# Seven products of halves instead of eight in the up-projections of a ConvFFN, on one Trainium2 core

## The chip, the cores and the metric

The kernel runs on one core of one Trainium2 chip. The metric is the time of one execution in microseconds of device time. Times of stretches are counted from the first instruction of the profiled execution.

## The reference, cut to what matters

Two layers (a hybrid of attention and linear attention, then a short convolution) process 512 prompt tokens and 32 sample tokens, 544 columns together. Each layer ends in a ConvFFN, and this is where the change lies:

```python
D_FF = ((8 * D_MODEL // 3 + 127) // 128) * 128     # 2816, D_MODEL = 1024

def conv_ffn(h, w_up, conv_w, conv_b, w_down, past):
    u = h @ w_up                                   # (tokens, 2 * D_FF)
    uc, new = causal_dwconv(u, past, conv_w)       # three taps along the tokens
    gate, val = jnp.split(uc + conv_b, 2, axis=-1)
    return (jax.nn.gelu(gate, approximate=True) * val) @ w_down, new
```

## The kernel before

Features lie on partitions, tokens along the free axis, in float32. Each product is made as three matmuls of float32r: weights and activations are split into a high part (`wh`, `xh`) and the rest (`wl`, `xl`), and high by high, high by low and low by high are summed in PSUM (`mm3`). The tokens are two halves of 256 and 288 columns.

Weights come in jobs of 128 x 1024 floats: SP issues the DMA into `wr`, ACT copies to `wh` (L193), DVE subtracts to get `wl` (L196); `prepare` runs two jobs ahead of the products.

The ConvFFN (`ffn`, L1546) has 22 pairs of a gate block and a value block of 128 features each. They are done in parts of 5, 5, 4, 4 and 4 pairs (`PARTS`). In a part, the up-projection of each pair runs (two jobs of 48 matmuls each, `run`), its epilogue `ev` multiplies by the norm, does the three taps on ACT and DVE (L1580 to L1582), the gelu, the product of gate and value (L1589) and its split (L411, L412) into `gh` and `gl`. Then the down-projection of the part runs over these: eight blocks, whose contraction goes over the pairs of the part. So the first matmuls of a down-projection need the first pair's `gh` and `gl`, the last ones of each block the last pair's.

The tensor engine's products use five PSUM banks (`pg`). POOL (GpSimd) only prepares margins: it clears and fills the history columns of `u` (L1569, L1570) and copies out the new state (L1578), and it adds squares for the norms.

The order on each engine is set at build time by the framework's scheduler. An engine then works through its instructions in that order; each waits for its operands and holds up those behind it.

Of the kernel before, what the change touches and what calls it, by code (L numbers as in the profile page):

```python
# [32 lines left out]
PARTS = (5, 5, 4, 4, 4)  # L33
# [52 lines left out]
def tile_hybrid_step(  # L86
# [65 lines left out]
    def sm_(w=256, s="m"):  # L152
        return apool.tile([P, w], F32, tag="m", name=nm(s), bufs=3)
# [27 lines left out]
    loaders = []  # L181
# [3 lines left out]

    def prepare(upto, eng=V):
        while len(wready) <= min(upto, len(loaders) - 1):
            n, load = loaders[len(wready)]
            wr = wpool.tile([P, 8 * P], F32, tag="wr", name=nm("wr"), bufs=2)
            wl = wpool.tile([P, 8 * P], F32R, tag="wl", name=nm("wl"))  # L190
            wh = wpool.tile([P, 8 * P], F32R, tag="wh", name=nm("wh"))
            load(wr)
            ins = S.activation(wh[:, :n], wr[:, :n], AF.Copy)  # L193
            if hold:
                behind(ins, hold[0])
            ins = eng.tensor_tensor(wl[:, :n], wr[:, :n], wh[:, :n].bitcast(F32), ALU.subtract)  # L196
            if vhold and eng is V:
                behind(ins, vhold[0])
            if load is load_glr:
                wk, lk = (t.rearrange("p (k c) -> p k c", k=8) for t in (wh, wl))  # L200
                eng.tensor_copy(wk[:, :, 16:32], lk[:, :, 0:16])
            wready.append((wh, wl))

    def cols(w, c0, r0=0, nkb=8):
        n = 2 * P if nkb == 4 else P

        def load(wr):
            nc.sync.dma_start(
                wr[:, : nkb * n].rearrange("p (k c) -> p k c", k=nkb),
                w[r0 : r0 + nkb * P, c0 : c0 + n].rearrange("(k p) c -> p k c", p=P),  # L210
            )
# [24 lines left out]
    def behind(ins, first):  # L236
        """keeps ins behind first in its engine's order"""
# [7 lines left out]
    def fence(ins, us):  # L245
        """ins goes ahead of the products that come more than us microseconds from here"""
# [29 lines left out]

# [1511 lines left out]
```

## Time and profile before

| | |
|---|---|
| time, median of 3 runs | 1328.41 us (1327.65 to 1331.36) |
| span of the profiled execution, first to last instruction | 1323.4 us |
| its own time outside the span | not listed; the median is 5.0 us above the span |
| PE / DVE / ACT / POOL busy | 97% / 63% / 42% / 18% |

PE is TensorE's matmuls, DVE is VectorE, ACT is ScalarE, POOL is GpSimd. In a timeline the first column is the start, the second the duration; where a row has "x2", both instructions are in one row. The distance between the starts of two instructions that follow each other without idle time is what one costs its engine.

### The profile page before, as it was taken

Reading aid. Unit: us, or ns where it says so; the run is one execution under the profiler, and the core shown is the slowest. Engines: PE = TensorE matmul, PEld = TensorE weight load, DVE = VectorE, ACT = ScalarE, POOL = GpSimd, SP = SyncE. Lnnn points to the kernel's source line nnn. Section 1 sums busy time; section 2 is a strip of 40 time slices with the busy share of each in tenths; the row PEclk is TensorE's granted clock in tenths of the full one; section 3 lists DMA queues with packets and bytes.
Section 4 is the critical chain, followed back from the end, with each engine's and each line's share of the span. In section 5 each row is a group of like instructions: output and inputs, shape, how many; then the busy total and the mean of one; then the engine's idle time right before and its main releaser. Section 6 shows DMA issues by size and latency. Waiting matters only on the chain.

```text
span 1323.4 us, 25024 instructions
## 1 busy us (share of the span) xinstructions
PE 1290.0 (97%) x10094; PEld 1253.5 (95%) x10094; DVE 839.3 (63%) x1692; ACT 561.8 (42%) x1070; POOL 233.9 (18%) x469
## 2 busy tenths in 40 slices
PE   7999999989999999999998999998999999999997
PEld 6999887888999999999998999998999999999997
DVE  6487466477837657575778645428755656657566
ACT  6555456644543334242445322335444323333244
POOL 4110210153301001020244000035120101001013
PEclk9999999999999999999999999999999999999999
DMA  6422221222242242323221432321333233232311
GB/s 213 112 51 67 85 74 35 68 64 75 61 138 73 76 125 80 96 80 96 80 81 39 120 96 80 103 70 37 104 89 112 61 107 105 81 96 80 96 45 69
DMA packets 199982, 113.14 MB, mean 85 GB/s; under 512 B 13805, under 2 KB 198218, under 8 KB 199850
## 3 DMA queue, kind: packets, MB, share of 16 engines
q1 hardware_dynamic: 194114, 106.99, 27.7%
q10 hardware_dynamic: 5304, 3.38, 0.8%
q8 instruction: 79, 1.29, 0.4%
q0 software_dynamic: 448, 1.18, 0.3%
q14 instruction: 37, 0.30, 0.1%
HBM read 107.07 MB, written 5.47 MB: 85 GB/s over the span
## 4 chain that ended last, share of the span: by engine, by line
PE 90%; DVE 7%; issue 1%; DMA 0%; POOL 0%; ACT 0%; SPq 0%; POOLq 0%; DVEq 0%; ACTq 0%
PE pg L225 27%; PE pg L230 27%; PE pg L232 27%; DVE m L536 2%; DVE xl L552 2%; PE ps L178 2%; DVE xres L540 2%; PE ps L1240 1%; PE ps L968 1%; PE ps L1301 1%; DMA sink<-attn_sinks 0%; PE ps L306 0%; DVE m L491 0%; PE ps L318 0%; PE ps L1178 0%
## 5 line engine op out<-in xcount | busy, mean ns | idle before, releaser
L225 PE MATMUL pg<-xh,wh 128*128 128x256 f32 (+1 forms) x2048 | 593.0, 291 | 5.3 <-DVE m L491 3.6
L230 PE MATMUL pg<-xl,wh 128*128 128x256 f32 (+1 forms) x2048 | 592.1, 289 | 2.8 <-DVE xl L552 2.4
L232 PE MATMUL pg<-xh,wl 128*128 128x256 f32 (+1 forms) x2032 | 586.4, 289 | 0.0
L225 PEld LDWEIGHTS pg<-xh,wh 128*128 128x128 f32 x2048 | 387.1, 190 | 8.4 <-issue 5.4
L230 PEld LDWEIGHTS pg<-xl,wh 128*128 128x128 f32 x2048 | 388.0, 189 | 4.4 <-DVE xl L552 3.0
L232 PEld LDWEIGHTS pg<-xh,wl 128*128 128x128 f32 x2032 | 384.2, 189 | 1.0 <-issue 0.9
L193 ACT ACTIVATE wh<-wr 128x1024 fp32r<-128x1024 f32 (+1 forms) x203 | 204.5, 1009 | 375.2 <-PE pg L230 272.2
L196 DVE TENSOR_TENSOR wl<-wr,wh 128x1024 fp32r<-128x1024 f32 (+1 forms) x197 | 228.1, 1159 | 142.4 <-ACT wh L193 140.7
L230 PE MATMUL pg<-gl,wh 128*128 128x256 f32 (+1 forms) x704 | 200.8, 288 | 0.0
L232 PE MATMUL pg<-gh,wl 128*128 128x256 f32 (+1 forms) x704 | 200.3, 288 | 0.0
L225 PE MATMUL pg<-gh,wh 128*128 128x256 f32 (+1 forms) x704 | 195.4, 289 | 0.0
L1578 POOL COPY uc<-u 128x18 f32<-128x18 f32 x88 | 51.7, 588 | 602.5 <-DVE u L1577 602.5
L230 PEld LDWEIGHTS pg<-gl,wh 128*128 128x128 f32 x704 | 132.3, 188 | 0.2
L232 PEld LDWEIGHTS pg<-gh,wl 128*128 128x128 f32 x704 | 132.3, 188 | 0.0
L225 PEld LDWEIGHTS pg<-gh,wh 128*128 128x128 f32 x704 | 129.1, 188 | 0.0
L1574 DVE TENSOR_TENSOR u<-pg,nbc 128x256 f32<-128x256 f32 x88 | 36.8, 423 | 113.6 <-PE pg L232 113.6
L491 DVE TENSOR_TENSOR m<-m,pg 128x256 f32<-128x256 f32 (+1 forms) x144 | 58.8, 434 | 57.1 <-PE pg L232 56.8
L1580 ACT ACTIVATE y<-u,cw 128x560 f32<-128x560 f32 x88 | 74.1, 849 | 20.2 <-DVE u L1577 20.1
L411 ACT ACTIVATE gh<-y 128x512 fp32r<-128x512 f32 x88 | 33.0, 423 | 102.1 <-DVE y L1589 52.5
L1582 DVE SCALAR_TENSOR_TENSOR y<-u,cw,y 128x560 f32<-128x560 f32 x88 | 70.1, 801 | 2.5
L1581 DVE SCALAR_TENSOR_TENSOR y<-u,cw,y 128x560 f32<-128x560 f32 x88 | 69.6, 797 | 1.4 <-ACT y L1580 1.0
L1584 ACT ACTIVATE y<-y 128x560 f32<-128x560 f32 x44 | 29.5, 671 | 66.8 <-DVE y L1582 66.5
(297 smaller groups left out, 1583.7 us busy)
## 6 DMA issues: line engine op xcount, KB each, us to landing
wr<-ffn_up SPq DMA_DIRECT2D x88, 512.0 KB, 3.8
wr<-ffn_down SPq DMA_DIRECT2D x24, 512.0 KB, 3.4
wr<-w_in_odd SPq DMA_DIRECT2D x24, 512.0 KB, 3.8
wr<-ffn_down SPq DMA_DIRECT2D x32, 320.0 KB, 3.2
wr<-w_in_even SPq DMA_DIRECT2D x14, 512.0 KB, 3.8
wr<-w_out_odd SPq DMA_DIRECT2D x8, 512.0 KB
xt<-x_prompt SPq DMA_DIRECT2D x4, 512.0 KB, 4.1
wr<-w_in_even SPq DMA_DIRECT2D x8, 256.0 KB, 3.7
```

The lines of the kernel that those rows point to most:

```text
L193: ins = S.activation(wh[:, :n], wr[:, :n], AF.Copy)
L196: ins = eng.tensor_tensor(wl[:, :n], wr[:, :n], wh[:, :n].bitcast(F32), ALU.subtract)
L225: ins = PE.matmul(ps[:, :n], lhsT=wh, rhs=xh[kb][:, sl], start=first, stop=False)
L230: PE.matmul(ps[:, :n], lhsT=wh, rhs=xl[kb][:, sl], start=False, stop=last and packed)
L232: PE.matmul(ps[:, :n], lhsT=wl, rhs=xh[kb][:, sl], start=False, stop=last)
L411: S.activation(h, src, AF.Copy)
L491: V.tensor_tensor(self.m[m][:, sl], self.m[m][:, sl], ps[:, :n], ALU.add)
L1574: V.tensor_tensor(u[:, 2:258], ps[:, 0:256], bc[:, 0:256], ALU.mult)
L1578: G.tensor_copy(ucv[:, :, :, c], u[:, TP : TP + 54].rearrange("p (g k) -> p g k", k=6)[:, :, 0:2])
L1580: S.activation(y[:, 0:560], u[:, 2:562], AF.Identity, scale=cv(2, c), bias=cv(3, c))
L1581: V.scalar_tensor_tensor(y[:, 0:560], u[:, 1:561], cv(1, c), y[:, 0:560], ALU.mult, ALU.add)
L1582: V.scalar_tensor_tensor(y[:, 0:560], u[:, 0:560], cv(0, c), y[:, 0:560], ALU.mult, ALU.add)
```

## The change

For the pairs of parts 1 to 5 (`PARTS` is now 4, 4, 4, 4, 4, 2; part 0 still uses eight products), contraction, tokens and the pair of blocks are each cut in two, and the resulting 2 x 2 by 2 x 2 product is made in seven products of halves instead of eight (Strassen's scheme in Winograd's form). A product is four steps of contraction by three matmuls of 272 columns. Four sums of weight blocks per pair are made on POOL (`quads`), the sums of activations once a layer in part 0 (`sums` during its up-projection, `plain` during its down-projection), and the seven results are put together in `pair` with ACT, DVE and POOL. Weights come in units of 128 x 512 floats everywhere, with eight raw buffers and ten split ones.

```diff
-PARTS = (5, 5, 4, 4, 4)
+PARTS = (4, 4, 4, 4, 4, 2)
+UN = 4 * P
+MID = T // 2
...
-    wpool = ctx.enter_context(tc.tile_pool(name="wpool", bufs=5))
+    wpool = ctx.enter_context(tc.tile_pool(name="wpool", bufs=10))
...
+    def quads(w, c1, c2):
+
+        t = {}
+
+        def add(k, x, y, op):
+            t[k] = wpool.tile([P, UN], F32, tag="ws", name=nm("ws"), bufs=3)
+            in_turn("sum", G.tensor_tensor(t[k], t[x], t[y], op))
+
+        def first():
+            for k, r0, c0 in (("11", 0, c1), ("21", 0, c2), ("22", 4 * P, c2), ("12", 4 * P, c1)):
+                t[k] = unit(w, r0, c0)()
+            return t["11"]
+
+        def second():
+            add("s1", "21", "22", ALU.add)
+            add("s2", "s1", "11", ALU.subtract)
+            return t["s2"]
+
+        def fifth():
+            add("s3", "11", "21", ALU.subtract)
+            return t["s3"]
+
+        def sixth():
+            add("s4", "12", "s2", ALU.subtract)
+            return t["s4"]
+
+        return [first, second, lambda: t["s1"], lambda: t["12"], fifth, sixth, lambda: t["22"]]
...
+    def product(ps, xs, first, ahead=8):
+
+        u = nxt[0]
+        nxt[0] += 1
+        prepare(u + ahead)
+        xh, xl = zip(*xs)
+        for kb in range(4):
+            mm3(ps, wready[u], kb, xh, xl, kb, MID, slice(0, MID), first and kb == 0, kb == 3)
...
+        def normed(c, sl):
+            x = tt(s="xn")
+            V.scalar_tensor_tensor(x[:, sl], xres[c][:, sl], gcol(2, l, c), bc[:, sl], ALU.mult, ALU.mult)
+            return x
...
+        def sums(k):
+            xa, xb = normed(k, slice(0, T)), normed(k + 4, slice(0, T))
+            u = tt(s="xu")
+            G.tensor_tensor(u[:, lo_h], xa[:, hi_h], xa[:, lo_h], ALU.subtract)
+            G.tensor_tensor(u[:, hi_h], xb[:, hi_h], u[:, lo_h], ALU.subtract)
+            keep(at(F32R, s="qh"), at(F32R, s="ql"), u, ("t1", k), ("t2", k))
+            if k % 2 == 0:
+                third[0] = tt(s="xv")
+            v = third[0][:, (lo_h, hi_h)[k % 2]]
+            G.tensor_tensor(v, xb[:, hi_h], xa[:, hi_h], ALU.subtract)
+            if k % 2 == 1:
+                keep(at(F32R, s="qh"), at(F32R, s="ql"), third[0], ("t3", k - 1), ("t3", k))
+
+        def plain(k):
+
+            xa, xb = normed(k, slice(0, T)), normed(k + 4, slice(0, T))
+            keep(xh[k + 4], xl[k + 4], xb, ("21", k), ("22", k))
+            d = ht()[:, :MID]
+            G.tensor_tensor(d, xb[:, lo_h], xb[:, hi_h], ALU.subtract)
+            G.tensor_tensor(xa[:, hi_h], xa[:, hi_h], xa[:, lo_h], ALU.subtract)
+            G.tensor_tensor(xa[:, hi_h], xa[:, hi_h], d, ALU.add)
+            keep(xh[k], xl[k], xa, ("11", k), ("t4", k))
...
+        def pair(c):
+
+            h = slice(0, MID)
+            pa, pb, pc, pd = bank(), bank(), bank(), bank()
+            p1, p5, u2, u3 = ht(), ht(), ht(), ht()
+            ua, ub = open_u(c), open_u(FC + c)
+            product(pa, xq["11"], True)
+            S.activation(p1[:, h], pa[:, h], AF.Copy)
+            product(pb, xq["t2"], True)
+            V.tensor_tensor(u2[:, h], pb[:, h], p1[:, h], ALU.add)
+            product(pc, xq["t1"], True)
+            S.activation(p5[:, h], pc[:, h], AF.Copy)
+            product(pa, xq["21"], False)
+            S.activation(ua[:, 2 : 2 + MID], pa[:, h], AF.Copy)
+            product(pb, xq["t3"], False)
+            V.tensor_tensor(u3[:, h], pb[:, h], p1[:, h], ALU.add)
+            product(pc, xq["22"], False)
+            n = TP - MID
+            V.tensor_tensor(ua[:, 2 + MID : 2 + TP], pc[:, :n], u2[:, :n], ALU.add)
+            V.tensor_tensor(smp(ua)[:, :, 2:6], tv(pc, n), tv(u2, n), ALU.add)
+            conv(c)
+            product(pd, xq["t4"], True)
+            G.tensor_tensor(ub[:, 2 + MID : 2 + TP], u3[:, :n], p5[:, :n], ALU.add)
+            G.tensor_tensor(smp(ub)[:, :, 2:6], tv(u3, n), tv(p5, n), ALU.add)
+            V.tensor_tensor(ub[:, 2 : 2 + MID], pd[:, h], u3[:, h], ALU.add)
+            conv(FC + c)
```

`keep` splits a sum into its high part (ACT) and its rest (DVE); `conv` is the old epilogue from the taps on.

How the order on the engines moves, at three places. First, DVE in layer 0 at the end of part 0, of the kernel before: the taps of the last value block (`y658`), its product with the gate and the split `gl660`, which the last contraction step of the down-projection needs.

```order
L1582 SCALAR_TENSOR_TENSOR y651_4101<-u650_4094,cw471_2945,y651_4101 128x560
L1574 TENSOR_TENSOR u657_4162<-pg655_4112,nbc534_3181 128x256
L1576 TENSOR_TENSOR u657_4162<-pg656_4113,nbc534_3181 128x256
L1577 TENSOR_TENSOR u657_4162<-pg656_4113,nbc534_3181 128x8x4
L196 TENSOR_TENSOR wl672_4262<-wr671_4261,wh673_4263 128x640
L1581 SCALAR_TENSOR_TENSOR y658_4169<-u657_4162,cw471_2945,y658_4169 128x560
L1582 SCALAR_TENSOR_TENSOR y658_4169<-u657_4162,cw471_2945,y658_4169 128x560
L1589 TENSOR_TENSOR y651_4101<-y651_4101,y658_4169 128x512
L1590 TENSOR_TENSOR y651_4101<-y651_4101,y658_4169 128x8x4
L412 TENSOR_TENSOR gl660_4174<-y651_4101,gh659_4173 128x512
```

The same place of the changed kernel; `xn` are the normed activations of `plain` (L1702), `xl` their new rests (L501), `gl795` the split of the last pair.

```order
L1702 SCALAR_TENSOR_TENSOR xn817_4474<-xres2_92,gv_98,nbc635_3385 128x544
L501 TENSOR_TENSOR xl626_3376<-xn801_4382,xh618_3368 128x544
L1702 SCALAR_TENSOR_TENSOR xn818_4476<-xres6_96,gv_98,nbc635_3385 128x544
L501 TENSOR_TENSOR xl631_3381<-xn810_4430,xh623_3373 128x544
L1702 SCALAR_TENSOR_TENSOR xn825_4520<-xres3_93,gv_98,nbc635_3385 128x544
L1690 TENSOR_TENSOR y783_4262<-y783_4262,y793_4336 128x512
L1691 TENSOR_TENSOR y783_4262<-y783_4262,y793_4336 128x8x4
L1702 SCALAR_TENSOR_TENSOR xn826_4522<-xres7_97,gv_98,nbc635_3385 128x544
L501 TENSOR_TENSOR xl627_3377<-xn809_4428,xh619_3369 128x544
L501 TENSOR_TENSOR xl632_3382<-xn818_4476,xh624_3374 128x544
L501 TENSOR_TENSOR xl628_3378<-xn817_4474,xh620_3370 128x544
L501 TENSOR_TENSOR gl795_4341<-y783_4262,gh794_4340 128x512
```

The last pair's split now stands behind work of `plain` that the down-projection of part 0 doesn't need.

Second, DVE in a pair. Before, in part 1, one weight rest of 1024 columns stands between the epilogues of two blocks:

```order
L1574 TENSOR_TENSOR u722_4700<-pg720_4650,nbc534_3181 128x256
L412 TENSOR_TENSOR gl716_4637<-y707_4564,gh715_4636 128x512
L412 TENSOR_TENSOR gl716_4637<-y707_4564,gh715_4636 128x32
L1576 TENSOR_TENSOR u722_4700<-pg721_4651,nbc534_3181 128x256
L1577 TENSOR_TENSOR u722_4700<-pg721_4651,nbc534_3181 128x8x4
L196 TENSOR_TENSOR wl741_4856<-wr740_4855,wh742_4857 128x1024
L1581 SCALAR_TENSOR_TENSOR y723_4707<-u722_4700,cw471_2945,y723_4707 128x560
L1582 SCALAR_TENSOR_TENSOR y723_4707<-u722_4700,cw471_2945,y723_4707 128x560
```

Of the change, in part 1, from `u3` of its second pair to `u2` of the third (`h` are `p1`, `u2`, `u3`; `ws` are sums of weights from POOL):

```order
L1754 TENSOR_TENSOR h907_4878<-pg901_4872,h904_4875 128x272
L202 TENSOR_TENSOR wl931_5010<-wr927_5002,wh932_5011 128x512
L1757 TENSOR_TENSOR u908_4879<-pg902_4873,h906_4877 128x240
L1758 TENSOR_TENSOR u908_4879<-pg902_4873,h906_4877 128x8x4
L1763 TENSOR_TENSOR u909_4882<-pg903_4874,h907_4878 128x272
L202 TENSOR_TENSOR wl948_5060<-ws947_5058,wh949_5061 128x512
L202 TENSOR_TENSOR wl950_5077<-ws946_5056,wh951_5078 128x512
L1682 SCALAR_TENSOR_TENSOR y926_4997<-u908_4879,cw559_3121,y926_4997 128x560
L1682 SCALAR_TENSOR_TENSOR y933_5030<-u909_4882,cw559_3121,y933_5030 128x560
L1683 SCALAR_TENSOR_TENSOR y926_4997<-u908_4879,cw559_3121,y926_4997 128x560
L202 TENSOR_TENSOR wl952_5094<-wr930_5008,wh953_5095 128x512
L1748 TENSOR_TENSOR h942_5048<-pg937_5043,h940_5046 128x272
```

A pair has seven rests of 512 columns in place of two of 1024, and they stand between the instructions that free PSUM banks.

Third, POOL in layer 0. Before, in part 0:

```order
L1569 MEMSET u625_3876 128x2
L1570 COPY u625_3876<-stT477_2960 128x8x2
L1578 COPY uc584_3466<-u625_3876 128x18
L1569 MEMSET u634_3951 128x2
L1570 COPY u634_3951<-stT477_2960 128x8x2
```

Of the change, in the second pair of part 1:

```order
L1679 COPY uc691_3682<-u859_4683 128x18
L1679 COPY uc691_3682<-u858_4680 128x18
L1661 MEMSET u908_4879 128x2
L1662 COPY u908_4879<-stT566_3138 128x8x2
L1661 MEMSET u909_4882 128x2
L1662 COPY u909_4882<-stT566_3138 128x8x2
L249 TENSOR_TENSOR ws921_4959<-wr894_4837,ws911_4887 128x512
L249 TENSOR_TENSOR ws946_5056<-wr928_5004,wr929_5006 128x512
L249 TENSOR_TENSOR ws947_5058<-ws946_5056,wr927_5002 128x512
L249 TENSOR_TENSOR ws954_5111<-wr927_5002,wr928_5004 128x512
L1761 TENSOR_TENSOR u909_4882<-h907_4878,h905_4876 128x240
L1762 TENSOR_TENSOR u909_4882<-h907_4878,h905_4876 128x8x4
```

Between the small copies POOL now has four sums of 512 columns and two additions for the value block in each pair.

## Rows read from the trace of the kernel before

**Rows 1.** The page: span, busy time by engine, chain that ended last.

```profile
span 1323.4 us, 25024 instructions
...
PE 1290.0 (97%) x10094; PEld 1253.5 (95%) x10094; DVE 839.3 (63%) x1692; ACT 561.8 (42%) x1070; POOL 233.9 (18%) x469
...
PE 90%; DVE 7%; issue 1%; DMA 0%; POOL 0%; ACT 0%; SPq 0%; POOLq 0%; DVEq 0%; ACTq 0%
```

**Rows 2.** Windows: length, then PE, PEld, DVE, ACT, POOL busy, clock, DMA.

```profile
331.00:662.00 331.00, 331.00 (x2653) 330.93 (x2652) 213.12 (x390) 125.07 (x180) 42.78 (x114) 1.00 0.31 91
...
340.00:353.00 13.00, 13.00 (x107) 13.00 (x106) 12.77 (x29) 6.62 (x14) 7.27 (x9) 1.00 0.26 78
...
352.70:387.30 34.60, 34.60 (x279) 34.60 (x278) 13.29 (x18) 14.85 (x29) 1.06 (x3) 1.00 0.41 117
```

**Rows 3.** PE timeline: two matmuls twelve apart, and the first of a down-projection.

```profile
440.36 0.28 PE L225 MATMUL pg<-xh,wh 128*128 128x256 f32 x1
...
441.86 0.28 PE L225 MATMUL pg<-xh,wh 128*128 128x256 f32 x1
...
352.71 0.28 PE L225 MATMUL pg<-gh,wh 128*128 128x256 f32 x1
```

**Rows 4.** DVE timeline in part 0, without idle time between the rows.

```profile
343.13 0.69 DVE L1589 TENSOR_TENSOR y<-y,y 128x512 f32<-128x512 f32 x1
343.73 0.19 DVE L1590 TENSOR_TENSOR y<-y,y 128x32 f32<-128x32 f32 x1
343.83 0.42 DVE L1576 TENSOR_TENSOR u<-pg,nbc 128x256 f32<-128x256 f32 x1
344.16 0.19 DVE L1577 TENSOR_TENSOR u<-pg,nbc 128x32 f32<-128x32 f32 x1
344.26 0.80 DVE L1582 SCALAR_TENSOR_TENSOR y<-u,cw,y 128x560 f32<-128x560 f32 x1
344.97 0.82 DVE L196 TENSOR_TENSOR wl<-wr,wh 128x640 fp32r<-128x640 f32 x1
345.71 0.79 DVE L412 TENSOR_TENSOR gl<-y,gh 128x512 fp32r<-128x512 f32 x2
```

**Rows 5.** DVE timeline: first taps of part 0, last split of part 0.

```profile
326.49 0.18 DVE L1577 TENSOR_TENSOR u<-pg,nbc 128x32 f32<-128x32 f32 x1
326.59 1.51 DVE L1581 SCALAR_TENSOR_TENSOR y<-u,cw,y 128x560 f32<-128x560 f32 x2
...
357.54 0.79 DVE L412 TENSOR_TENSOR gl<-y,gh 128x512 fp32r<-128x512 f32 x2 [0.66 <-ACT gh L411]
```

**Rows 6.** Groups on POOL by shape: busy us, mean ns, idle before.

```profile
L1578 POOL COPY uc<-u 128x18 f32<-128x18 f32 x88 | 51.7, 588 | 602.5 <-DVE u L1577 602.5
...
L196 POOL TENSOR_TENSOR wl<-wr,wh 128x1024 fp32r<-128x1024 f32 x6 | 15.1, 2512 | 7.9 <-ACT wh L193 7.9
```

**Rows 7.** POOL and DVE timelines ahead of part 0, where both are at work.

```profile
274.52 2.66 POOL L196 TENSOR_TENSOR wl<-wr,wh 128x1024 fp32r<-128x1024 f32 x1 [0.62 <-ACT wh L193]
...
291.54 5.10 POOL L424 TENSOR_TENSOR nss<-nss,h 128x256 f32<-128x256 f32 x6
...
275.20 2.26 DVE L552 SCALAR_TENSOR_TENSOR xl<-xres,gv,xh 128x256 fp32r<-128x256 f32 x1
...
293.37 1.76 DVE L536 SCALAR_TENSOR_TENSOR m<-m,gv,pbc 128x288 f32<-128x288 f32 x2 [2.74 <-ACT pbc L321]
295.05 0.99 DVE L540 TENSOR_TENSOR xres<-xres,m 128x288 f32<-128x288 f32 x1
295.96 0.99 DVE L536 SCALAR_TENSOR_TENSOR m<-m,gv,pbc 128x288 f32<-128x288 f32 x1
296.88 0.45 DVE L540 TENSOR_TENSOR xres<-xres,m 128x288 f32<-128x288 f32 x1
297.25 0.51 DVE L552 SCALAR_TENSOR_TENSOR xl<-xres,gv,xh 128x288 fp32r<-128x288 f32 x1
297.68 0.51 DVE L536 SCALAR_TENSOR_TENSOR m<-m,gv,pbc 128x288 f32<-128x288 f32 x1
```

More of the change, by code (lines that the diff above doesn't have):

```diff
@@ new lines, in tile_hybrid_step, with in_turn, unit, load @@
+    turn = {}
+    def in_turn(what, ins):
+        if what in turn:
+            behind(ins, turn[what])
+        turn[what] = ins
+    def unit(w, r0, c0, nkb=4):
+        def load():
+            wr = raw_tile()
+            ins = nc.sync.dma_start(
+                wr.rearrange("p (k c) -> p k c", k=nkb),
+                w[r0 : r0 + nkb * P, c0 : c0 + UN // nkb].rearrange("(k p) c -> p k c", p=P),
+            )
+            in_turn("load", ins)
+            return wr
+        return load
@@ L249, in tile_hybrid_step, with run, at_unit @@
     late = []
-    def run(jobs, order, ahead=2, hook=None, tick=None, spare=()):
+    def run(jobs, order, ahead=4, hook=None, tick=None, spare=()):
         base = nxt[0]
-        per = 2 if jobs[0][0] == 4 else 1
-        nxt[0] += len(jobs) // per
+        nkb = jobs[0][0]
+        per = 2 if nkb == 2 else 1
+        nu = max(1, nkb // 4)
+        nxt[0] += nu * len(jobs) // per
+        def at_unit(j, kb):
+            if per == 2:
+                return base + j // 2, kb * 2 + j % 2
+            return base + j * nu + kb // 4, kb % 4
         for grp in order:
-            prepare(base + max(j for j, _ in grp) // per + ahead)
+            prepare(at_unit(max(j for j, _ in grp), nkb - 1)[0] + ahead)
             pss = []
@@ L359, in tile_hybrid_step @@
+            return wr
+        return load
+    units += cols(wi, KB)
+    units += [load_glr(0), load_glr(4 * P)]
     for o in (KB + P, QB, QB + P, VB, VB + P, VB + 2 * P, VB + 3 * P, VA, KA):
[L360 to L366 removed]
+        units += cols(wi, o)
@@ L1418, in step @@
             if hook:
[L1419 removed]
+                run(js, [[(j, hf) for j in range(n) for hf in range(2)]], 4, hook)
             else:
[L1421 removed]
+                run(js, halves(n), 6, tick=paced)
         def drain():
@@ L1606, in ffn, with tick @@
+                def tick():
+                    if len(todo) > 0:
+                        k = todo.pop(0)
+                        if k is not None:
+                            sums(k)
+                run(jobs, FIRST4 + seq(len(jobs) - 5, 5), spare=SPARE, tick=tick)
+            else:
+                for c in range(c0, c0 + n):
+                    pair(c)
             last = pi == len(PARTS) - 1
@@ L1616, in ffn, with tick2 @@
                     odd_rows()
-            run([(n, gh, gl, post.ev(m, pi == 0, last)) for m in range(8)], ALL8 if last else seq(8))
+            rest = list(range(4)) if pi == 0 else []
+            def tick2():
+                if rest:
+                    plain(rest.pop(0))
+            run([(n, gh, gl, post.ev(m, pi == 0, last)) for m in range(8)], ALL8 if last else seq(8), tick=tick2)
     def out_states(uc, dst_p, dst_s, n0):
```

265 lines of the change are left out of this document (147 added, 118 removed).

## The prediction, made before the changed kernel had run

> **What bounds the kernel now.** I read the page first: PE is busy 1290.0 of 1323.4 us, and 90% of the chain that ended last is PE [rows 1]. So the place is found by windows. From 331 to 662 us, the up- and down-projections of layer 0, PE has no gap at a clock of 1.00, while DVE is busy 213 of 331 us and POOL 43 [rows 2]. The share of DVE hides a tide: from 340 to 353, while up-projections run, it is busy 12.8 of 13.0 us, and in the 34.6 us of the first down-projection 13.3 [rows 2]. What frees matmuls is therefore worth its full time only as long as DVE has what PE needs in time, stage by stage.
>
> **What the change removes.** Twelve matmuls start in 441.86 - 440.36 = 1.50 us, half of them of 256 columns, half of 288, so one of 272 on average costs 0.125 us [rows 3]. A pair takes 96 of them in its up-projection before and 7 x 4 x 3 = 84 after. Eighteen pairs in each of two layers lose 12 each: 432 matmuls, which the order confirms, or 432 x 0.1247 = **53.9 us** off PE. The number of down-projection matmuls stays.
>
> **What DVE does instead.** Its prices are distances of starts [rows 4]: 0.60 us for 512 columns from SBUF, 0.33 for 256 from PSUM (0.35 for 272, 0.32 for 240, in proportion), 0.71 for a tap of 560, 0.10 for 32 columns. By the slope from 512 to 640 columns (0.74), 544 columns cost 0.64, and a scaled one 0.70.
>
> *Parts 1 to 4.* In the order of the change, between the first `u2` and the last split of a part of four pairs, DVE has 27 weight rests (16.2 us), 16 taps (11.4), 8 gate products and splits (4.8), 12 additions of 272 (4.2), 4 of 240 (1.3) and 12 small ones (1.2): **39.1 us**. PE's 336 matmuls take 41.9 us, so that alone would just fit.
>
> *Part 0.* Its up-projection is that of four old pairs. PE reached the down-projection at 352.7 with five pairs [rows 3]; two jobs of 48 matmuls less make it 340.7. DVE begins the taps at 326.6 [rows 5], after the evictions that wait for the norm's second half, which nothing in the change brings forward. From there to `gl795`, the last pair's split, the order has 16 normed activations (11.1 us), 12 rests of 544 (7.6), 16 taps (11.4), 7 weight rests (4.2), 8 products and splits (4.8), 6 evictions (2.0) and 10 small ones (1.0): 42.1 us, so 368.7 at the earliest. Before, the last split began at 357.5, 4.8 us after the down-projection [rows 3, 5], and PE never waited. Now five banks are all that PE can open: in its order 47 matmuls (5.9 us) stand ahead of the first that needs the last pair. It is out of work at 346.6, and waits at least **22.1 us in each layer**.
>
> **POOL in DVE's way.** The trace of before has no such load in an FFN part, so its cost is bounded. A POOL operation on 256 columns takes 5.10/6 = 0.85 us [rows 7], on 1024 columns 2.51 [rows 6]: 1.40 for a sum of 512, 0.89 for 272, 0.82 for 240, 0.37 for 32. While POOL added squares without a pause, from 293.37 to 296.64, four DVE instructions took 3.51 us that undisturbed cost 0.43 + 0.37 + 0.43 + 0.43 = 1.66: 0.57 us lost per us of POOL [rows 7]. The upper bound is the instruction that began at 275.20, 0.68 us into POOL's 2.66: it took 2.26 instead of some 0.40, 0.94 per us of what was left [rows 7]. The lower bound is nothing, as for small copies of 0.2 us. I take 0.57, times 0.85 for DVE's evictions from PSUM, which show no such stretch: **0.48**.
>
> The Trainium skill (SBUF — State Buffer, section "Who interferes with whom") says that a DVE instruction with two SBUF inputs and a GpSimd instruction that reads SBUF exclude each other: the later one is blocked until the first is done. By that rule the loss is near my upper bound, a rival below; the row at 275.20 agrees with it, the run from 293.37 shows that less is lost when short ones alternate. The Trainium skill (GPSIMD Engine Reference, section "Instruction dispatch") gives about 2.5 cycles an element as the floor of a two-input operation, an estimate of 1.07 us for 512 columns; with that for a sum the total below would come out some 18 us lower.
>
> Per part of four, 12 of the 16 sums (by the order, four fall into the down-projection) and four additions with their samples are 12 x 1.40 + 4 x 1.19 = 21.6 us, a loss of 10.4. DVE needs 3.0 (until two products are done) + 39.1 + 10.4 = 52.5 us; PE has 41.9 and 5.6 more from five banks with three of four contraction steps: a wait of **5.0 us** (nothing at loss 0; 14.9 at 0.94). In the part of two: 3.0 + 19.6 + 5.2 against 21.0 + 1.9, a wait of **4.9** (0 to 9.9). In part 0, 3 weight sums and 21 operations of 272 columns stand ahead of `gl795`: 22.9 us of POOL, a loss of 11.0, so PE waits **33.1** (22.1 to 43.6).
>
> **Other edits cost nothing here.** SP issues 187 more, smaller loads; at a DMA share of 0.31 [rows 2] and with eight raw buffers they are hidden behind PE. ACT has five more weight copies a pair, though shorter ones, and three evictions; it was busy 125 of 331 us [rows 2]. Units of 512 outside the FFN cost DVE 0.03 us each, hidden by PE. Were a cover gone, a late load would show as a PE wait of some us at a part's start, which the range holds. After part 0 the DVE is free for the rest of the down-projection, so `plain` isn't late for part 1.
>
> **The sum.** Two layers of 33.1 + 4 x 5.0 + 4.9 = 58.0 are 116.0 us of waits against 53.9 saved: +62 us. The span was 1323.4 and the median 1328.4, so 5.0 us lie around the span, which I keep: 1328.4 + 62.1 = **1390 us**. With no loss to POOL it is 1328.4 - 53.9 + 44.2 = 1319; at 0.94 it is 1328.4 - 53.9 + 226 = 1500.
>
> **The rivals.** (1) *PE stays fed* and the saving comes whole: 1328.4 - 53.9 = 1275, the other side. For it: PE has no gap today even where DVE is busy 98% [rows 2]. Against it: `gl795` would have to be there by 346.6, so 42 us of DVE work in 20. Should half of part 0's DVE work be done while PE still runs the up-projection and before the taps, it would hold. Chance 0.12. (2) *POOL costs DVE nothing*, only part 0 waits: 1319, 1305 to 1335. For it: small copies did no harm; against it, every stretch of [rows 7]. Chance 0.18. (3) *The lock is whole*, 0.94 or more: 1440 to 1500. For it: the instruction at 275.20; against it: not all POOL work meets a DVE instruction. Chance 0.15. My forecast, 1335 to 1440, has 0.55.
>
> A difference under 0.3% (4 us) can't be told from no change here. Faster by more: rival 1 and half of rival 2, 0.21; within it 0.05; slower 0.74. The range of 8 in 10, 1310 to 1450, leaves out rival 1 and the end of rival 3; the forecast's own is 1335 to 1440.
>
> **What would show it.** Right: 432 matmuls less; PE idle 22 to 44 us in each layer inside part 0's down-projection, released by DVE's L501; PE waits of 3 to 8 us in each later up-projection, released by DVE; weight rests of 512 columns (L202) longer than 0.69 us on average while POOL makes sums; DVE above 85% busy in the up-projections. Wrong: PE without gaps in the FFN, which is rival 1; gaps in part 0 alone, with rests of undisturbed length, rival 2; rests well over 1 us, rival 3. A PE that waits for ACT, for POOL's sums themselves or for a load would make the mechanism wrong even at the right time.

## The result, and the profile after

The changed kernel takes 1445.96 us (median of 4 runs, 1443.91 to 1446.04), the kernel before 1329.88 beside it (4 runs, 1327.65 to 1332.0). The ratio is 1.087 (95% interval 1.085 to 1.089): slower by 116 us where +62 was forecast. The time lies inside the range of 1310 to 1450, at its upper end, and above the forecast's own 1335 to 1440.

The page of the profiled execution, to be read against [rows 1]: span, busy time, the chain that ended last, and the groups of the weight rests (L202) and weight sums (L249); a group ends in busy us, mean ns | idle time ahead.

```profile
span 1444.2 us, 26072 instructions
...
PE 1283.8 (89%) x9662; PEld 1236.1 (86%) x9662; DVE 1093.8 (76%) x2030; ACT 694.2 (48%) x1493; POOL 562.0 (39%) x740
...
PE 63%; DVE 28%; issue 5%; ACT 2%; DMA 1%; POOL 1%; ACTq 0%; SPq 0%; DVEq 0%; POOLq 0%
...
L202 DVE TENSOR_TENSOR wl<-wr,wh 128x512 fp32r<-128x512 f32 x334 | 271.2, 822 | 99.4 <-ACT wh L198 84.2
...
L202 DVE TENSOR_TENSOR wl<-ws,wh 128x512 fp32r<-128x512 f32 x144 | 125.3, 879 | 24.2 <-ACT wh L198 16.5
L249 POOL TENSOR_TENSOR ws<-wr,ws 128x512 f32<-128x512 f32 x36 | 59.3, 1648 | 190.0 <-issue 106.5
...
L249 POOL TENSOR_TENSOR ws<-wr,wr 128x512 f32<-128x512 f32 x72 | 115.4, 1603 | 42.1 <-DMA wr<-ffn_up 22.2
```

PE has 10094 - 9662 = 432 matmuls less, yet its busy time fell by 6.2 us only. DVE's share of the chain rose from 7 to 28%, its busy time by 254.5 us. A rest takes 0.82 to 0.88 us.

Windows: length, then PE, PEld, DVE, ACT, POOL busy, granted clock, DMA. The first row is a whole part of four of the kernel before, for comparison; all others are of the changed kernel. Of these, the first three are part 0 of layer 0, the fourth runs from the first `u2` of part 1 to its last split, the last is one whole part of four, from the last matmul of one down-projection to the last of the next.

```profile
472.50:544.50 72.00, 72.00 (x578) 71.96 (x577) 46.25 (x85) 24.73 (x32) 7.49 (x24) 1.00 0.32 96
...
340.00:360.00 20.00, 8.12 (x54) 7.90 (x52) 20.00 (x31) 8.62 (x15) 12.14 (x14) 0.74 0.14 41
360.00:380.00 20.00, 8.55 (x41) 7.11 (x39) 20.00 (x29) 7.81 (x13) 13.33 (x18) 0.61 0.05 13
...
329.80:387.10 57.30, 28.38 (x180) 26.37 (x178) 57.30 (x77) 23.51 (x39) 38.86 (x41) 0.71 0.11 33
...
410.50:463.35 52.85, 46.15 (x362) 45.20 (x360) 51.33 (x80) 30.23 (x58) 31.47 (x43) 1.00 0.35 100
...
558.20:633.10 74.90, 69.07 (x531) 68.06 (x531) 65.37 (x105) 36.18 (x68) 39.07 (x48) 0.98 0.29 85
```

Before, PE had no idle time from 331 to 662 us [rows 2]. Now DVE is the engine without gaps in part 0, where PE is busy 28 of 57 us, in good part at the lower of its clocks (1.2 instead of 2.4 GHz). The timeline of PE shows where it waited (idle time and releaser in brackets), first part 0, then the seam of part 1:

```profile
354.63 0.61 PE L277 MATMUL pg<-xh,wh 128*128 128x288 f32 x1 [11.88 <-DVE u L1669]
...
371.45 0.58 PE L282 MATMUL pg<-gl,wh 128*128 128x256 f32 x1 [3.64 <-DVE gl L501]
382.81 1.49 PE L277 MATMUL pg<-gh,wh 128*128 128x256 f32 x5 [8.75 <-ACT gh L500]
387.08 0.58 PE L282 MATMUL pg<-gl,wh 128*128 128x256 f32 x1 [2.78 <-DVE gl L501]
...
454.82 0.39 PE L277 MATMUL pg<-gh,wh 128*128 128x256 f32 x1 [2.18 <-DVE h L1754]
...
462.57 0.89 PE L277 MATMUL pg<-gh,wh 128*128 128x256 f32 x5 [3.42 <-ACT gh L500]
```

ACT is named where `gh` came last, but ACT itself waited for DVE's gate product (L1690), which stands at the end of the pair's work on DVE. The timeline of ACT shows its wait in part 1; the timeline of DVE shows the product, and what answers to [rows 5]:

```profile
461.89 0.75 ACT L500 ACTIVATE gh<-y 128x512 fp32r<-128x512 f32 x2 [0.84 <-DVE y L1690]
...
329.80 0.80 DVE L1682 SCALAR_TENSOR_TENSOR y<-u,cw,y 128x560 f32<-128x560 f32 x1
...
380.79 1.24 DVE L1690 TENSOR_TENSOR y<-y,y 128x512 f32<-128x512 f32 x1
381.96 0.74 DVE L1691 TENSOR_TENSOR y<-y,y 128x32 f32<-128x32 f32 x1
382.62 0.77 DVE L1702 SCALAR_TENSOR_TENSOR xn<-xres,gv,nbc 128x544 f32<-128x544 f32 x1
383.32 3.11 DVE L501 TENSOR_TENSOR xl<-xn,xh 128x544 fp32r<-128x544 f32 x3
386.35 0.79 DVE L501 TENSOR_TENSOR gl<-y,gh 128x512 fp32r<-128x512 f32 x2
...
450.26 3.45 DVE L202 TENSOR_TENSOR wl<-wr,wh 128x512 fp32r<-128x512 f32 x2
...
461.17 0.69 DVE L1690 TENSOR_TENSOR y<-y,y 128x512 f32<-128x512 f32 x1
461.77 0.19 DVE L1691 TENSOR_TENSOR y<-y,y 128x32 f32<-128x32 f32 x1
462.55 0.80 DVE L501 TENSOR_TENSOR gl<-y,gh 128x512 fp32r<-128x512 f32 x2 [0.59 <-ACT gh L500]
```

The first taps start 3.2 us later than in [rows 5], the last split of part 0 at 386.35 instead of 357.54. The two rests at 450.26 take 3.45 us in place of 1.3: POOL was adding weights.

**Where the time went.** The account is kept by the last matmuls of the down-projections; those of part 0 in layer 0, before and after the change:

```profile
382.60 0.29 PE L232 MATMUL pg<-gh,wl 128*128 128x288 f32 x1
...
407.03 0.30 PE L284 MATMUL pg<-gh,wl 128*128 128x288 f32 x1
```

A part of four took 72.0 us before; with 48 matmuls less (6.0 us) it would take 66.0, a part of two 33.0, and part 0 would end at 382.6 - 18.0 = 364.6 (a pair is 72.0 / 4). It ended at 407.0, late by 42.4 us; in layer 1 the way from the end of layer 0 to the end of part 0 is 43.5 longer. The eight parts of four took 74.8 to 75.6 us, 72.9 too much in all, the two parts of two 41.4 and 41.2, 16.6 too much. What follows the last down-projection grew from 13.4 to 19.2 us, and 6.0 of what the last parts of before had lost themselves is in these numbers already. The sum, 42.4 + 43.5 + 72.9 + 16.6 + 5.8 - 6.0 = 175.2, is, within 0.5, the growth of the span plus the saving, 120.8 + 53.9 = 174.7. The medians grew by 116 only, because the profiled execution of before was 3 to 5 us faster than the medians: in every run that lists both, a span is 1.8 us shorter than its execution, so 1323.4 belongs to a time of 1325.2.

### The profile page after: what moved, and what is told of

Its sections match the earlier page's. It is cut to its first block, busy times and chain, and to the rows that moved or that the text cites. A ratio compares the mean times of both kernels' runs of the same rounds, so it can differ in the third digit from the quotient of the medians.

```text
span 1444.2 us, 26072 instructions
## 1 busy us (share of the span) xinstructions
PE 1283.8 (89%) x9662; PEld 1236.1 (86%) x9662; DVE 1093.8 (76%) x2030; ACT 694.2 (48%) x1493; POOL 562.0 (39%) x740
## 4 chain that ended last, share of the span: by engine, by line
PE 63%; DVE 28%; issue 5%; ACT 2%; DMA 1%; POOL 1%; ACTq 0%; SPq 0%; DVEq 0%; POOLq 0%
PE pg L282 18%; PE pg L277 18%; PE pg L284 18%; DVE wl L202 6%; DVE y L1683 4%; DVE y L1682 3%; DVE m L625 2%; DVE y L1690 2%; DVE xn L1702 2%; PE ps L180 1%; DVE gl L501 1%; DVE xres L629 1%; PE ps L1061 1%; PE ps L1394 1%; DVE xl L501 1%
## 5 line engine op out<-in xcount | busy, mean ns | idle before, releaser
L277 PE MATMUL pg<-xh,wh 128*128 128x256 f32 (+2 forms) x1472 | 425.9, 294 | 30.1 <-DVE u L1669 23.9
L282 PE MATMUL pg<-xl,wh 128*128 128x256 f32 (+2 forms) x1472 | 426.1, 291 | 0.6 <-DVE xl L641 0.6
L284 PE MATMUL pg<-xh,wl 128*128 128x272 f32 (+2 forms) x1456 | 420.4, 291 | 0.0
L202 DVE TENSOR_TENSOR wl<-wr,wh 128x512 fp32r<-128x512 f32 x334 | 271.2, 822 | 99.4 <-ACT wh L198 84.2
L198 ACT ACTIVATE wh<-wr 128x512 fp32r<-128x512 f32 x346 | 212.6, 626 | 248.0 <-PE pg L282 229.0
L202 DVE TENSOR_TENSOR wl<-ws,wh 128x512 fp32r<-128x512 f32 x144 | 125.3, 879 | 24.2 <-ACT wh L198 16.5
L249 POOL TENSOR_TENSOR ws<-wr,ws 128x512 f32<-128x512 f32 x36 | 59.3, 1648 | 190.0 <-issue 106.5
L580 DVE TENSOR_TENSOR m<-m,pg 128x256 f32<-128x256 f32 (+1 forms) x176 | 75.1, 436 | 75.4 <-PE pg L284 74.4
L249 POOL TENSOR_TENSOR ws<-wr,wr 128x512 f32<-128x512 f32 x72 | 115.4, 1603 | 42.1 <-DMA wr<-ffn_up 22.2
L277 PE MATMUL pg<-qh,wh 128*128 128x272 f32 x432 | 125.0, 289 | 2.9 <-DVE h L1748 2.9
L282 PE MATMUL pg<-ql,wh 128*128 128x272 f32 x432 | 124.3, 288 | 0.0
L284 PE MATMUL pg<-qh,wl 128*128 128x272 f32 x432 | 124.3, 288 | 0.0
```

Source lines behind the costliest of these rows:

```text
L198: ins = S.activation(wh, src, AF.Copy)
L202: ins = eng.tensor_tensor(wl, src, wh.bitcast(F32), ALU.subtract)
L249: in_turn("sum", G.tensor_tensor(t[k], t[x], t[y], op))
L580: V.tensor_tensor(self.m[m][:, sl], self.m[m][:, sl], ps[:, :n], ALU.add)
```

## The experiments

The theory: DVE ends the waits. In part 0 it has the activations' preparation ahead of the last split; in the other parts POOL's weight sums slow its two-operand instructions; PE pays. The rivals: DVE's own additional work is enough, whatever POOL does; the clock is a cost of its own; or POOL's lateness with the sums holds things up. Times below are medians; the changed kernel's is 1446.0, the kernel before took 1327.5 to 1329.2 beside them.

**1. No weight sums.**

```diff
-        return [first, second, lambda: t["s1"], lambda: t["12"], fifth, sixth, lambda: t["22"]]
+        return [first, lambda: t["21"], lambda: t["22"], lambda: t["12"], lambda: t["11"], lambda: t["12"], lambda: t["22"]]
```

> Leaves out the four sums of weight tiles per pair: their places are taken by the raw tiles, so ACT's seven roundings and DVE's seven remainders per pair stay, and the 144 subtractions on POOL are gone. Contention theory (POOL's sums slow the remainders on DVE, DVE then starves TensorE): the remainders L202 fall from a mean of 0.82 to 0.88 us back to about 0.69 us, the period of a part of four falls from 75 us to 66 to 69 us, that of a part of two from 41 to 33 to 36 us, and the time from 1446 to between 1355 and 1380 us. Rival (DVE's own additional instructions are enough, whatever POOL does): the remainders get shorter but the parts keep periods of 73 us or more, and the time stays above 1430 us. Part 0 stays late by 30 us or more per layer under both.

Measured: 1378.9 us, ratio 1.038 (1.032 to 1.043). Busy time and rests from its groups, and windows from first `u2` to last split of part 1, and of one whole part:

```profile
PE 1260.7 (92%) x9662; PEld 1218.7 (89%) x9662; DVE 993.1 (72%) x2030; ACT 695.8 (51%) x1493; POOL 323.5 (24%) x596
```

```profile
L202 DVE TENSOR_TENSOR wl<-wr,wh 128x512 fp32r<-128x512 f32 x478 | 327.2, 695 | 147.0 <-ACT wh L198 131.3 <-PE pg L284 3.3 <-DMA swa_v_p<-vtk 2.6
```

```profile
406.16:452.50 46.34, 45.42 (x363) 45.14 (x361) 41.37 (x79) 30.38 (x58) 12.16 (x32) 1.00 0.40 114
...
538.00:605.50 67.50, 66.56 (x530) 66.28 (x529) 53.77 (x105) 36.43 (x68) 12.18 (x32) 1.00 0.33 94
```

DVE does the same 2030 instructions in 100.7 us less; the sums had kept POOL busy for 228.7 (59.3, 115.4, and 54.0 of a third group). That is 0.44 us lost per us of POOL. A part of four takes 67.5 us, and PE's clock in it is 1.00. Part 0 stays 38.1 us late in layer 0 and 40.0 in layer 1. The rival of DVE's own work falls for the parts of four. For the parts of two the expectation missed: they stay at 41.4 and 40.8 us.

**2. No preparation of the activations.** `sums` and `plain` do nothing; the products read halves of `xh` and `xl`.

```diff
-                            sums(k)
+                            halves_of_x(k)
...
-                    plain(rest.pop(0))
+                return
```

> Leaves out the sums of activations and the new splits of the plain halves in part 0: the seven products read halves of the normed rows that are there anyway. The theory that part 0's order on DVE is a term of its own: part 0's down-projection ends about 40 us earlier in each layer, the parts of four keep their 75 us, and the time falls from 1446 to between 1360 and 1375 us. Rival (the late part 0 is already the contention with the weight sums, which begin there): part 0 stays late by 15 us or more, and the time stays above 1390 us.

Measured: 1383.3 us (ratio 1.041, 1.035 to 1.047). Part 0 is late by 10.1 us in layer 0 instead of 42.4, by 11.1 instead of 43.5 in layer 1; the last split is there at 356.14. The parts of four take 73.3 to 76.6 us. So the preparation makes 32 us of the loss in each layer, less than the 40 of the theory, and the time lies above the theory's 1375 as it lies below the rival's 1390: 10 us of lateness have another cause.

**3. Neither.**

> Leaves out both the weight sums and the activations' preparation; the seven products with their evictions, ACT copies and remainders stay. If these two are the whole of the loss, the saved 53.9 us of TensorE show: between 1275 and 1300 us, and the two single savings add up to about this one's within 15 us. Rival (the smaller weight units, the banks, or the seven products' own evictions cost something of their own): 1310 us or more.

Measured: 1317.6 us, ratio 0.992 (0.990 to 0.995). The two savings add up (67.1 + 62.7 = 129.8 against 128.4), but the rival's 1310 is passed: without either preparation the seven products win 10 us of 53.9 (1327.5 beside them; by the spans of the profiled executions 6.7). From the same stages as above: part 0 is still late by 9.6 and 8.4 us, a part of four takes 67.5 (1.5 too much, eight times), the parts of two 42.3 and 41.1 (17.4 too much), the tail is 6.3 longer; less the 6.0 from above that is 47.7, where 1316.7 - (1323.4 - 53.9) = 47.2 are missing. What the part of two waits for stands in PE's timeline:

```profile
668.05 0.97 PE L180 MATMUL ps<-ident,uc 128*88 128x128 f32 x7 [0.63 <-POOL uc L1679]
672.60 1.44 PE L277 MATMUL pg<-gh,wh 128*128 128x256 f32 x5 [3.59 <-ACT gh L500]
```

With two pairs, few matmuls stand ahead of the last pair's split, and its chain (evictions, taps, gelu, product, split) shows. That reading is argued from the order; experiment 11 moves the part, but doesn't lengthen it.

**4. The sums on DVE.**

```diff
-            in_turn("sum", G.tensor_tensor(t[k], t[x], t[y], op))
+            in_turn("sum", V.tensor_tensor(t[k], t[x], t[y], op))
```

> The same computation as the changed kernel, but the 144 weight sums run on DVE instead of POOL. Contention theory: DVE gets 4 instructions of about 0.6 us per pair more (2.4 us, 86 us in all) and loses the slowed remainders (about 110 us in all: 478 remainders of 0.83 us in the mean, instead of 0.60 from start to start); the time is between 1400 and 1445 us. Rival (POOL's sums cost DVE nothing that matters): DVE is fuller by 86 us in the stages where TensorE already waits for it, and the time rises to between 1480 and 1530 us.

Measured: 1416.5 us, ratio 1.066 (1.061 to 1.071). Its page and groups:

```profile
PE 1274.1 (90%) x9662; PEld 1227.0 (87%) x9662; DVE 1081.7 (77%) x2174; ACT 698.8 (49%) x1493; POOL 332.3 (24%) x596
```

```profile
L202 DVE TENSOR_TENSOR wl<-ws,wh 128x512 fp32r<-128x512 f32 x144 | 97.9, 684 | 20.0 <-ACT wh L198 14.8 <-PE pg L284 2.6
...
L249 DVE TENSOR_TENSOR ws<-wr,wr 128x512 f32<-128x512 f32 x72 | 49.2, 683 | 0.6
```

DVE does 144 instructions more and is busy 12.1 us less. A sum takes 0.68 us there, and 1.59 on POOL, of which DVE loses 0.70. POOL's help costs DVE as much as the work itself. This is the experiment that shows contention with the computation unchanged; the parts of four fall to 70.8 to 72.3 us.

**5. POOL writes, but reads nothing.**

```diff
-            in_turn("sum", G.tensor_tensor(t[k], t[x], t[y], op))
+            in_turn("sum", G.memset(t[k], 0.01))
```

> Leaves out the weight sums, but POOL fills their tiles with a constant at the same places, so that ACT and DVE still wait for POOL and POOL still writes SBUF, but reads nothing. Theory (what slows DVE is POOL's reading of its two operands while DVE reads its own): the remainders L202 return to 0.68 to 0.71 us, the parts of four to 67 to 69 us, and the time is within 10 us of the run without weight sums (1379). Rival (what counts is that remainders wait for a tile that POOL makes, or that POOL writes SBUF at all): the remainders stay above 0.76 us or the parts above 72 us, and the time is 1410 us or more.

Measured: 1379.1 us, the time without sums.

```profile
PE 1261.6 (92%) x9662; PEld 1219.6 (89%) x9662; DVE 993.2 (72%) x2030; ACT 695.8 (51%) x1493; POOL 399.9 (29%) x740
```

DVE's busy time is that of experiment 1 to 0.1 us. Waiting for a tile of POOL's, or POOL's writing, costs nothing; the fills are shorter than the sums (0.53 us, 75.2 in all), so how late a tile is was not held equal.

**6. POOL reads one operand.**

```diff
-            in_turn("sum", G.tensor_tensor(t[k], t[x], t[y], op))
+            in_turn("sum", G.tensor_copy(t[k], t[x]))
```

> Leaves out the weight sums; POOL copies the first operand instead, so it reads one SBUF operand in place of two. Theory (any POOL instruction that reads SBUF keeps DVE's two-operand instructions off while it runs): DVE loses as much per us of POOL as beside the sums (0.44 to 0.48), so its busy time is above the 993 us of the run that only writes by 0.44 to 0.48 times the copies' time. Rival (only two-operand POOL instructions do it): DVE's busy time stays between 988 and 1000 us, the remainders at 0.69 us, and the time at 1379 us as with writes alone.

Measured: 1401.2 us (ratio 1.055, 1.052 to 1.058), neither the one nor the other.

```profile
PE 1270.1 (91%) x9662; PEld 1228.8 (88%) x9662; DVE 1021.7 (73%) x2030; ACT 696.3 (50%) x1493; POOL 456.2 (33%) x740
```

```profile
L249 POOL COPY ws<-wr 128x512 f32<-128x512 f32 x108 | 93.8, 869 | 225.0 <-DVE wl L202 205.9 <-DMA wr<-ffn_up 19.1
...
L249 POOL COPY ws<-ws 128x512 f32<-128x512 f32 x36 | 30.0, 833 | 56.0 <-DVE wl L202 55.5
```

DVE loses 1021.7 - 993.2 = 28.5 us to 123.8 of POOL: 0.23 per us, half of what it loses to the sums. Reading is what counts, and one operand does harm too. Why it does half the harm is taken up below.

**7. The kernel before with as many sums on POOL.**

```diff
+            if load in summed:
+                for k in (0, 512):
+                    ws = wpool.tile([P, 512], F32, tag="ws", name=nm("ws"), bufs=1)
+                    whf = wh.bitcast(F32)
+                    G.tensor_tensor(ws, whf[:, k : k + 512], whf[:, 512 - k : 1024 - k], ALU.add)
...
```

> The kernel before with 144 sums of 512 columns added on POOL, four to a pair in the pairs that the change turns into seven products; they read the rounded weight tiles, and nobody reads their results. DVE should lose 0.44 to 0.48 us per us of POOL, 100 to 110 us in all, so its busy time rises from 839 to 925 to 950 us. Theory (the loss counts only where DVE has less slack than that): at 63% busy DVE makes up for it, TensorE waits little, and the time is between 1328 and 1350 us. Rival (POOL's sums cost TensorE's time in any kernel, as the 66 us between the changed kernel and its run without sums suggest): 1370 us or more.

Measured: 1337.8 us, ratio 1.007 (1.005 to 1.010).

```profile
PE 1290.9 (97%) x10094; PEld 1252.6 (94%) x10094; DVE 902.0 (68%) x1692; ACT 557.0 (42%) x1070; POOL 491.3 (37%) x613
```

The time is as the theory has it; DVE's loss is not: 902.0 - 839.3 = 62.7 us for 269.0 us of sums, 0.23 per us. The trace shows why. During 125 of the changed kernel's 144 sums a DVE instruction with two operands in SBUF starts, here during 73 of 144; such a meeting costs DVE 0.8 to 0.9 us in both. Where DVE is less busy, more of POOL's time meets nothing. As many sums as cost the changed kernel 67 us cost 9 here.

**8. The plain halves behind the last split.**

```diff
...
             ins = V.scalar_tensor_tensor(x[:, sl], xres[c][:, sl], gcol(2, l, c), bc[:, sl], ALU.mult, ALU.mult)
+            if after_gl[0] is not None:
+                behind(ins, after_gl[0])
...
             rest = list(range(4)) if pi == 0 else []
+            after_gl[0] = last_gl[0]
```

> The same computation as the changed kernel; only the order on DVE differs: the normed activations and splits of the plain halves stand behind the last pair's split in part 0. Order theory: the split of the last pair, at 386.35 us in the changed kernel, comes about 12 us earlier, part 0's down-projection ends about 10 us earlier per layer, and the time falls from 1446 to between 1421 and 1431 us. Rival (the same work is only moved, and part 1 then waits for its plain halves): part 0's down-projection ends earlier, part 1's first product starts with a wait of 8 us or more, and the time stays between 1438 and 1452 us.

Measured: 1425.1 us, ratio 1.072 (1.069 to 1.075). DVE's timeline (L1704 is the normed activation):

```profile
372.19 0.79 DVE L501 TENSOR_TENSOR gl<-y,gh 128x512 fp32r<-128x512 f32 x2 [0.65 <-ACT gh L500]
372.90 8.78 DVE L1704 SCALAR_TENSOR_TENSOR xn<-xres,gv,nbc 128x544 f32<-128x544 f32 x8
```

The last split comes 14.2 us earlier, part 0 ends 13.2 us earlier, and part 1 takes 78.7 us instead of 75.6. The order accounts for some 10 us per layer.

**9. TensorE kept busy in its waits.**

```diff
+                if warm and grp is order[0] and kb == nkb - 1:
+                    keep_busy(wready[base][0], jobs[0][1][0], warm)
...
```

> Adds 20 matmuls of 256 columns, whose result nobody reads, in front of the first matmuls that wait for the last pair in the down-projections of parts 1 to 5: some 2.4 us of work in waits of 2 to 3.6 us. Clock theory (a part of the loss is that TensorE runs at half clock for 3.4 us after each such wait, 1.7 us a part): the stretches at half clock behind these waits vanish, and the time falls by 10 to 17 us, from 1446 to between 1429 and 1436 us. Rival (the waits are set by DVE alone, the clock takes nothing): the added matmuls are hidden or cost up to 2 us a part, and the time is between 1444 and 1466 us.

Measured: 1446.3 us (ratio 1.088, 1.085 to 1.091): no change. But the parts of four took 73.1 to 74.2 us, 12.2 less in all, and the parts of two 50.2 and 44.4, 12.0 more. In PE's timeline of the part of two the added matmuls (L346) came behind the wait, not in it, and a second wait followed:

```profile
729.32 0.99 PE L277 MATMUL pg<-gh,wh 128*128 128x256 f32 x4 [3.60 <-ACT gh L516]
731.93 0.41 PE L180 MATMUL ps<-ident,rows 128*128 128x128 f32 x1
731.99 3.11 PE L346 MATMUL ps<-gh,wh 128*128 128x256 f32 x20
744.68 1.01 PE L391 MATMUL ps<-ones,pss 128*128 128x1 f32 x4 [3.90 <-DVE pss L529]
```

So the run could not decide, and was repeated without them there.

**10. The same in the parts of four alone** (`warm=20 if 0 < pi and n == 4 else 0`).

> As the run with the 20 added matmuls, but without them in the part of two pairs, where they cost 9 and 3 us and the half clock came all the same. Clock theory: parts 1 to 4 keep their periods of 73 to 74 us against 75.2, the part of two its 41.4, and the time is between 1430 and 1437 us. Rival (what the parts of four win is given back behind them): 1442 us or more.

Measured: 1433.5 us, ratio 1.080 (1.078 to 1.083). One whole part in windows:

```profile
553.80:626.90 73.10, 70.36 (x550) 68.93 (x549) 64.73 (x105) 36.51 (x68) 41.43 (x48) 1.00 0.30 88
```

The clock is 1.00 where it was 0.98, and a part takes 1.6 us less although PE does 20 matmuls more. DVE was not helped: the last split comes 55.4 to 56.2 us after the part's start, as in the changed kernel (55.5 to 56.3). What follows it takes 17.7 to 17.8 us instead of 19.2 to 19.3. The clock costs this in each of the eight parts, and 12.5 us of the time.

**11. The part of two fifth, a part of four last** (`PARTS = (4, 4, 4, 4, 2, 4)`).

> The same computation as the changed kernel with the part of two pairs fifth and a part of four last. Theory for the 5.8 us behind the last down-projection (19.2 us against 13.4 before): two pairs are too short a down-projection to hide the end of the evictions and sums of squares behind; with four pairs last, the rest behind it returns to 13 to 15 us and the time falls by 4 to 8 us, to between 1437 and 1442 us. Rival (the tail has to do with the changed pools, not with the last part's size): it stays at 18 us or more and the time within 3 us of 1446.

Measured: 1436.2 us, ratio 1.080 (1.077 to 1.084). The last matmul of the down-projection starts at 1422.2 of 1435.3 us, so what follows takes 13.1, as before the change (13.4). The time is 1 us below what the theory expected; the parts of two take 42.7 and 42.8 us in their new place, 1.5 more.

**12. Four repairs together** (4, 8, 10 and 11).

> The same computation as the changed kernel with four repairs together: the weight sums on DVE, the plain halves behind the last split in part 0, the part of two pairs fifth, and the 20 added matmuls in the parts of four. If the single gains add up (30, 21, 10, and up to 12 us), 1373 to 1390 us, still 45 us or more above the kernel before, because DVE then has the sums to do itself. Rival (the gains are of the same wait and don't add): 1395 us or more.

Measured: 1381.5 us, ratio 1.040 (1.038 to 1.042). The gains of the single runs make 72.7 us, together they are 64.5. A part of four takes 70.8 us (73.0 the last of each layer), 1.2 less than before the change, and part 0 is still late by 31 us in layer 0 and 24 in layer 1.

## Why the prediction was right in kind and short in size

- **The saving of PE** was 432 matmuls, as said. Its worth of 53.9 us never showed: even with neither preparation, 10 us were left (experiment 3).
- **Part 0, 33.1 us forecast, 42.4 and 43.5 measured.** That DVE's preparation ahead of the last split makes PE late was right: experiments 2 and 8 show the preparation as the cause of 32 us, its order of 10. The signs came half true. PE's waits in layer 0 are 28.9 us, but 17.0 of them stand in the down-projection, where 22 to 44 were expected, and 11.9 in the up-projection. L501 is named for 6.4 us, the evictions (L1669, L1672) for 13.6, and ACT's `gh` for 8.9. By the prediction's words a wait for ACT speaks against it; but ACT waited for DVE's L1690, so the chain is DVE's. The term was short by 9.3: DVE's taps began at 329.8, not at 326.6 (3.2: the last evictions ahead of them began 2.5 us later than before, and a normed activation stands between); its work up to the last split took 57.3 us, not 42.1 + 11.0 (4.2); and PE needed 19.9 us instead of 18.1 for the rest of the down-projection, part of it at 1.2 GHz (1.8). The wait of 11.88 us for the evictions of L1669, in the up-projection, was not foreseen. DVE had no gap from the first taps to the last split, so this wait adds nothing to the lateness that ends with that split.
- **Parts of four, 5.0 us forecast, 8.8 to 9.6 measured.** POOL's price came out near the forecast, at 0.44 us per us over all sums where 0.48 was taken. In part 1 DVE's busy time from first `u2` to last split is 51.3 us, where the sum had 39.1 + 10.4 = 49.5. Without the weight sums it is 41.4, which is what the sum's 39.1 and its 2.3 for POOL's additions, which stay there, make together. So the weight sums cost 10.0 where 8.1 of the 10.4 were theirs. What was short is DVE's path: with 3.5 us ahead of the first `u2` instead of 3.0, 1.8 more of work and 1.5 idle, the last split came 56.3 us after the part's start, not 52.5. And behind the split PE took 19.3 us where 17.7 to 17.8 are enough (experiments 1 and 10): the 1.5 us are the clock, which the sum had left out. Without weight sums the split comes after 49.8 us, still 1.5 later than a part of 66.0 allows; that is all that experiment 1 has left in these parts.
- **The part of two, 4.9 forecast, 8.4 and 8.2 measured,** and 5.8 us of tail not forecast. PE's idle time in it is 4.2 and 3.4 us, so the size of the wait was near, but from the wrong cause, by luck: without any sums the parts lose 8.4 and 7.8 us all the same (experiment 1). Of the rest, 6.0 us in both layers together is what the last parts of before had lost themselves, without idle time. The part's place at the end costs 10 us of time (experiment 11). That a junction with two pairs has too few matmuls to hide one pair's chain is argued.
- **The rivals.** PE fed (1275): not reached even without all preparation. POOL free of cost (1319): experiment 4 refutes it. The whole lock (1440 to 1500) has the measured time in its range, but not at its price: the mean loss was 0.44, not 0.94. That the range to 1450 held the time, by 4 us, was in part luck: it was reached through terms that the sum had at nothing, the clock (12.5 us), the tail (5.8) and a part 0 that is 10 us late without any preparation. The 5.0 us that the sum put around the span are 1.8; the rest was a fast execution in the profile.

In the forecast's terms, 66.2 + 40.0 + 9.8 = 116.0 us of waits stand against 85.9 + 72.9 + 16.6 = 175.4 of lateness measured. Part 0 was short by 19.7, the parts of four by 32.9, the parts of two by 6.8, of which 6.0 were there before.

The Trainium skill (SBUF — State Buffer, section "Who interferes with whom") says that a GpSimd instruction which only writes SBUF doesn't contend with a DVE instruction of two SBUF inputs, and that one which reads does. Experiment 5 agrees (0.1 us lost to 75.2 us of fills), and so do 4 and 6. It says too that the second to issue is blocked until the first is done. The trace of the changed kernel agrees, instruction by instruction:

```profile
425.01 1.73 POOL L249 TENSOR_TENSOR ws<-ws,wr 128x512 f32<-128x512 f32 x1 [1.63 <-issue]
427.36 1.66 POOL L249 TENSOR_TENSOR ws<-wr,wr 128x512 f32<-128x512 f32 x1 [0.63 <-DVE wl L202]
...
425.51 1.77 DVE L202 TENSOR_TENSOR wl<-ws,wh 128x512 fp32r<-128x512 f32 x1
427.21 0.68 DVE L1690 TENSOR_TENSOR y<-y,y 128x512 f32<-128x512 f32 x1
427.81 1.27 DVE L1691 TENSOR_TENSOR y<-y,y 128x32 f32<-128x32 f32 x1
```

The second sum ends at 429.02. L1690 was under way when it began, and takes its usual time. L1691, of 32 columns, starts during the sum, takes 1.27 us where 0.19 is usual, and ends 0.06 us after it. The sum in its turn ends 1.13 us after L1690; over all 144 sums the median is 1.15 us, counted from the end of the DVE instruction with two SBUF operands that was under way, or from the sum's own start where none was. So a POOL time of 1.59 us contains POOL's own wait for DVE, and the mean loss of 0.44 per us is a whole lock that some sums (19 of 144) miss and that lasts for a part of their time. A copy (experiment 6) holds DVE for less: its median, counted so, is 0.57 us, and 85 of 144 meet a DVE instruction with two operands in SBUF. DVE's instructions with one operand in PSUM lost nothing: those of L580 with 288 columns take 452 ns with the sums and 451 without (experiment 1).

The forecast had 1.40 us for a sum, and 1.07 as an estimate from the Trainium skill (GPSIMD Engine Reference, section "Instruction dispatch"). The second agrees with the 1.15 that a sum takes once it has what it reads, not with the 1.59 that it is seen to take beside a busy DVE.

Open: the traces show half of part 0's 10 us of lateness without preparation. In experiment 2 PE reaches its down-projection at 345.7, where the forecast had 340.7; it starts 2.2 us late behind a wait ahead of the FFN (287.6 instead of 285.4) and then waits 3.4 us for the sum of squares (`nss`), where it was 0.8. Why these come later, and what of the smaller weight units and the changed pools is in it, no run separates. Whether sums spread over more parts would fit is open too.

## What to carry to other kernels

Saving matmuls pays only while the engines that prepare operands and clear banks have slack in that very stage: here 10 us of 53.9 were left before a single sum was made. Work given to GpSimd is not free for VectorE when both read SBUF; price it as a loss on VectorE (0.23 to 0.44 us per us here, the more the busier VectorE is with instructions of two SBUF operands), and compare with doing it on VectorE outright. When a forecast has TensorE waiting some us at every seam, add the slower matmuls behind the wait, and look at the shortest part and at the last one, where the least work stands ahead of the chain.

## What the runs showed of the hardware that was not expected

- A sum of 512 columns cost VectorE 0.70 us of lost time while GpSimd did it in 1.59, and 0.68 when VectorE did it itself.
- The loss went with what GpSimd reads: 0.44 us per us for two operands, 0.23 for one, none for fills. By instruction it was a wait: one of 32 columns that started during a sum ended 0.06 us after it (1.27 us instead of 0.19).
- Twenty matmuls for nothing in each of eight waits made the kernel 12.5 us faster, with the granted clock at 1.00 instead of 0.95 to 0.98 in these parts.
